# Sparse attention with a convolution between its steps: attention steps given priority in the scheduler, one softmax scaling moved from GpSimd to VectorE, the first stage scheduled by the framework, a narrower last piece

## The chip, the cores and the metric

One core of a Trainium2 chip. The time is the device time of one execution in microseconds. The engines are TensorE (PE, with its weight loads as PEld), VectorE (DVE), ScalarE (ACT), GpSimd (POOL) and SyncE (SP), which here issues the DMAs.

## The reference

One step of a decoder layer for 1024 prompt tokens and 8 sample tokens with 1024 features, all in float32:

```python
shift, scale, gate = split(silu(c) @ w_ada + b_ada)
h = rmsnorm(x, g_pre) * (1 + scale) + shift
z = h @ w_in                     # 5912 columns: q, kv, gates, za, conv (B, C, x), cg, merge
# branch A, per head group: compressed, selected (top 16 blocks) and sliding-window attention
o_cmp = masked_softmax(q @ kc.T) @ vc
o_sel = masked_softmax(q @ k_sel.T) @ v_sel
o_win = masked_softmax(q @ k_win.T) @ v_win
o_attn = g0 * o_cmp + g1 * o_sel + g2 * o_win
ya = (o_attn * silu(za)) @ w_br_a
# branch B: short gated convolution
yb = (cb * conv3(cc * cx) * silu(cg)) @ w_br_b
o = (sigmoid(ga) * ya + sigmoid(gb) * yb) @ w_out
y = x + gate * rmsnorm(o, g_post)
```

With 1024 keys the prompt has 16 blocks of 64, so all blocks up to the current one are selected. Outputs are y of prompt and sample, the key and value rows, the window rows and the convolution state.

## The kernel before, in words

A float32 product is made of three matmuls on rounded halves: an operand a is split into ah (rounded, `copy`, L110 or L112) and al = a - ah (`sub`, L115), and ah·bh + al·bh + ah·bl go into one PSUM bank (`mm`, L106). PSUM has eight banks of 512 columns in four groups: two "acc", three "S", two "T", one "O".

**First stage (0 to about 75 us).** x comes in eight tiles of 128 tokens. `norm_x` squares and sums a tile on ACT and takes the inverse root on POOL, `scale_x` (L337) multiplies it on DVE, `trans_x` (L349) transposes it on PE, `ada` and `ada_end` make the modulation from `w_ada` as its pieces land, and `make_h` (L387 to L390, L112, L115) writes the halves Hh and Hl, feature by feature, for which projection matmuls of 344 columns wait. Up to `in_order.__exit__` (L739) a manual schedule (L285) holds all five engines to the order in which the code is written. This includes the projections of keys, values and queries and the compression of keys and values (G, L636, is a transposed piece of it; X its operand).

**Attention (231 to 595 us).** There are 16 pairs (eight query tiles of 128 by two key groups) with two units each, branch 1 (the compressed keys together with the selected ones) and branch 2 (the window). A unit's `a_steps` multiply queries by keys into an "S" bank, take mask and maximum on DVE (L963), the exponential on ACT (L968), then the sums' inverses and gates (L974 to L976), and scale the weights P: for the compressed part one POOL multiply of 128x256 (L979), for the others one multiply a head on DVE (L987) or, for the last head of a long row, on ACT. Its `b_steps` transpose P on PE into a "T" bank (L1000 for the compressed part, L1014 for the others), split it (ph on ACT L110, pl on DVE L115; pc for the compressed part) and multiply by the values into the pair's "O" bank, first `pc`. At the end of a pair the two halves of "O" are added into QO (L1033), the upper half by way of an SBUF tile `ot`.

**The filling.** The projections of the gated convolution (`conv_tiles`, three of its four blocks, 288 steps of three matmuls of 344 columns into "acc") are given out between the attention's steps: the loop at L1053 to L1090 sorts the a_steps of one unit and the b_steps of the unit before by their planned times, and ahead of each step `advance` takes as many filling steps as its share of the planned total. The filling's DVE work is at L862 to L882. Its last evaluation (`e_cg`) writes an SBUF tile `ct`. `ot` and `ct` share one slot (tag "tmp", one buffer), so each of them waits for the user before it in program order. Here the framework's scheduler sets the order on every engine from its own estimates, with the program order as the priority.

**After attention.** The fourth convolution block, the gates, both branch products, then w_out in eight tiles of 128 tokens with 48 matmuls of 512 columns each, and `finish` (L1351 to L1366) for each: squares and their sums on ACT (L1358), y = o·GG on DVE (L1359), mean and epsilon (L1360, L1361), the power -0.5 on POOL (L1362), y·st + x on DVE (L1365), two stores of 512 columns.

Of the kernel before, what the change touches and what calls it, by code (L numbers as in the profile page):

```python
# [19 lines left out]
F32 = mybir.dt.float32  # L20
F32R = mybir.dt.float32r
I32 = mybir.dt.int32
AF = mybir.ActivationFunctionType
OP = mybir.AluOpType
# [61 lines left out]
def _build(ctx, tc, nc, I, O):  # L86
# [3 lines left out]
    def dma(out, in_):  # L90
        return nc.sync.dma_start(out, in_)
# [7 lines left out]
    def bank(tag):  # L99
        return psum.tile([128, 512], F32, name="ps" + tag, tag=tag, bufs=NB[tag])  # L100
# [174 lines left out]
    def load_x(t):  # L275
# [4 lines left out]
        else:  # L280
# [1 line left out]
            dma(x, I["x_sample"][:, 0, :])  # L282
        xs[t] = x

    in_order = tc.manual_schedule(engines={mybir.EngineType.PE, mybir.EngineType.DVE, mybir.EngineType.Activation,  # L285
                                           mybir.EngineType.Pool, mybir.EngineType.SP})
    in_order.__enter__()
    dma(ct[0:1, :], I["c_prompt"])
    dma(ct[1:9, :], I["c_sample"])
# [654 lines left out]
    def a_steps(u):  # L944
        u.P, u.mx, u.sm = {}, [], []
        for br, n in u.parts:
            u.P[br] = ap.tile([128, 4, (64, 1024, 640)[br]], F32, name=f"P{br}", tag=f"P{br}", bufs=1)
            u.mx.append(ap.tile([128, 4, 2], F32, name="mx", tag="mx", bufs=3))
            u.sm.append(ap.tile([128, 8], F32, name="sm", tag="sm", bufs=3))
        K = KS[u.br - 1][u.g]  # L950
        hh = QT[u.i]
        for j in range(4):
            seen = [0] * len(u.parts)
            for k0, nt, subs in u.ch:
                ps = bank("S")
                mm(ps[:, :nt], hh[u.g][:, j, :], K[:, k0:k0 + nt], True, False)
                mm(ps[:, :nt], QL[u.g][:, j, :], K[:, k0:k0 + nt], False, True)
                c0 = 0
                for x, o, n, m in subs:
                    (br, total_n), mx, sm = u.parts[x], u.mx[x], u.sm[x]  # L960
                    Pb, ci = u.P[br], seen[x]
                    init = 0.1 * BIG if ci == 0 else mx[:, j, (ci - 1) % 2:(ci - 1) % 2 + 1]
                    V.tensor_tensor_reduce(out=Pb[:, j, o:o + n], in0=ps[:, c0:c0 + n], in1=m, scale=1.0, scalar=init,  # L963
                                           op0=OP.add, op1=OP.min, accum_out=mx[:, j, ci % 2:ci % 2 + 1])
                    seen[x] += 1
                    c0 += n
                    if o + n == total_n:
                        A.activation(Pb[:, j, 0:total_n], Pb[:, j, 0:total_n], AF.Exp, bias=mx[:, j, ci % 2:ci % 2 + 1], scale=-1.0,  # L968
                                     accum_out=sm[:, j:j + 1])
                if j == 3 and (k0, nt, subs) == u.ch[-1]:  # L970
                    for x, (br, n) in enumerate(u.parts):
                        sm, Pb = u.sm[x], u.P[br]
                        if br == 0:
                            V.tensor_scalar(sm[:, 0:4], sm[:, 0:4], 1e-30, None, op0=OP.max)  # L974
                        V.reciprocal(sm[:, 4:8], sm[:, 0:4])
                        V.tensor_tensor(out=sm[:, 4:8], in0=sm[:, 4:8],  # L976
                                        in1=gate[:, u.i, 12 * u.g + br:12 * u.g + br + 10:3], op=OP.mult)
                        if br == 0:
                            P.tensor_tensor(out=Pb, in0=Pb, in1=sm[:, 4:8].rearrange("p (j o) -> p j o", o=1).to_broadcast(  # L979
                                [128, 4, 64]), op=OP.mult)  # L980
                            continue
                        for jj in range(4):
                            p = Pb[:, jj, 0:n]
                            if jj == 3 and n > 256:
                                A.activation(p, p, AF.Copy, scale=sm[:, 4 + jj:5 + jj])
                            else:
                                V.tensor_scalar(p, p, sm[:, 4 + jj:5 + jj], None, op0=OP.mult)  # L987
                yield max(0.22, 2 * nt * 0.00046)
# [71 lines left out]
    for n in range(len(units) + 1):  # L1060
# [20 lines left out]
        for k, (at, which, t) in enumerate(ev):  # L1081
            if u:
                advance(span * (at - past))
                past = at
            next(lb if which else la)
        if u:
            advance(span * (1 - past))
        for _ in la:
# [201 lines left out]
    gps = tp.tile([128, D], F32, name="gps")  # L1290
    src = I["g_post"]
    dma(gps, bass.AP(tensor=src.tensor, offset=src.offset, ap=[[0, 128], [1, D]]))
    for b in range(2):
        cs = slice(512 * b, 512 * b + 512)
        ps = bank("S")
        mm(ps, kr[:, 0:128], gs2[:, cs], True, True)
        V.tensor_tensor(out=GG[:, cs], in0=ps, in1=gps[:, cs], op=OP.mult)
        ps = bank("S")
        mm(ps[:NS, :], kr[:, 128:136], gs2[:, cs], True, True)
        V.tensor_tensor(out=GS[:, cs], in0=ps[:NS, :], in1=gps[:NS, cs], op=OP.mult)  # L1300
# [47 lines left out]

    ob = pool("ob", "left")

    def finish(ps, n, x, g, dst):  # L1351

        sq = ob.tile([128, 512], F32, name="sq", tag="sq", bufs=1)
        st = ob.tile([128, 4], F32, name="fst", tag="fst", bufs=2)
        y = ob.tile([128, D], F32, name="y", tag="y", bufs=2)
        for h in range(2):
            cs = slice(512 * h, 512 * h + 512)
            A.activation(sq[:n], ps[h][:n, :], AF.Square, accum_out=st[:n, h:h + 1])  # L1358
            V.tensor_tensor(out=y[:n, cs], in0=ps[h][:n, :], in1=g[:n, cs], op=OP.mult)  # L1359
        V.tensor_tensor(out=st[:n, 2:3], in0=st[:n, 0:1], in1=st[:n, 1:2], op=OP.add)  # L1360
        V.tensor_scalar(st[:n, 2:3], st[:n, 2:3], 1.0 / D, EPS, op0=OP.mult, op1=OP.add)  # L1361
        P.tensor_tensor(out=st[:n, 3:4], in0=st[:n, 2:3], in1=mhalf[:n], op=OP.pow)  # L1362
        for h in range(2):
            cs = slice(512 * h, 512 * h + 512)
            V.scalar_tensor_tensor(y[:n, cs], y[:n, cs], st[:n, 3:4], x[:n, cs], op0=OP.mult, op1=OP.add)  # L1365
            dma(dst[:, cs], y[:n, cs])  # L1366


    msr = ob.tile([128, KT, 40], F32R, name="msr")
# [45 lines left out]
    for t in range(8):  # L1415
        if t < 7:
            split_m(t + 1)
        mh, ml = mt.pop(t)
        tag = "S" if t % 2 else "acc"
        ps = [bank(tag), bank(tag)]  # L1420
        for k0, k1 in (((0, 7), (7, 8)) if t == 0 else ((0, 8),)):
            for h in range(2):
                cs = slice(512 * h, 512 * h + 512)
                for k in range(k0, k1):
                    mm(ps[h], mh[k], WOh[:, k, cs], k == 0, False)
                    mm(ps[h], mh[k], WOl[:, k, cs], False, False)
                    mm(ps[h], ml[k], WOh[:, k, cs], False, k == KT - 1)
        if t == 1:
            sample_out()
        finish(ps, 128, xt.pop(t), GG, O["y_prompt"][0, 128 * t:128 * t + 128, :])  # L1430


_INS = ['x_prompt', 'x_sample', 'cache_kv_pages', 'state_win_kv', 'state_conv', 'page_table', 'c_prompt', 'c_sample',
# [22 lines left out]
```

## Time and profile before

| | us |
|---|---|
| three runs | 1085.88, 1086.84, 1087.47 |
| median | 1086.84 |
| the profiled execution: its own time | 1087.87 |
| its span, first to last instruction | 1086.1 |
| mean granted clock of TensorE | 0.985 of 2.4 GHz |

The page of the profile gives each engine's busy time and, in 40 slices of the span (27.15 us each), its busy share in tenths. A matmul's records overlap the next one's, so a busy PE shows no idle time but not the rate either; the rate is read from how many matmuls start in a stretch. "Waits" list for which other engine's instruction an idle engine waited.

### The profile page before, as it was taken

How to read it: one execution, taken by the hardware profiler on the slowest of the kernel's cores; microseconds unless marked ns; L12 is line 12 of the kernel's file. 1: busy time of each engine (PE TensorE's matmuls, PEld its weight loads, DVE VectorE, ACT ScalarE, POOL GpSimd, SP SyncE). 2: the span in 40 equal slices, each digit the busy share in tenths (PEclk: the TensorE clock that was granted, in tenths of full speed). 3: DMA queues.
4: the chain of work that ended last, by engine and by line, in shares of the span. 5: the costliest groups of instructions: out<-in, count | busy, mean ns of one | idle time of the engine just before them, and what ended most of it. 6: DMA issues, size and time to landing. Idle time of an engine off the chain costs nothing.

```text
span 1086.1 us, 17011 instructions
## 1 busy us (share of the span) xinstructions
PE 1043.6 (96%) x6310; PEld 959.7 (88%) x6310; DVE 673.4 (62%) x1823; ACT 453.4 (42%) x1006; POOL 105.3 (10%) x106
## 2 busy tenths in 40 slices
PE   5898999999999999999999999999999999999997
PEld 4688999978888988888888999999999999998785
DVE  4676656457998898878987745344365311583432
ACT  5566533346787767776666011111012111121221
POOL 3100000122222121211111010000000000120000
PEclk8899999989999999999999999999999999999999
DMA  9752242210000000000001312442331121332222
GB/s 329 209 146 76 78 101 59 70 30 20 21 20 20 21 20 20 11 20 11 20 21 42 98 51 65 154 128 61 79 81 46 40 58 40 105 108 79 79 78 78
DMA packets 103408, 75.98 MB, mean 70 GB/s; under 512 B 23873, under 2 KB 92680, under 8 KB 103324
## 3 DMA queue, kind: packets, MB, share of 16 engines
q1 hardware_dynamic: 103324, 74.88, 24.3%
q8 instruction: 50, 0.82, 0.3%
q14 instruction: 34, 0.28, 0.1%
HBM read 65.85 MB, written 9.01 MB: 69 GB/s over the span
## 4 chain that ended last, share of the span: by engine, by line
PE 60%; DVE 2%; ACT 0%; issue 0%; DVEq 0%; POOLq 0%; ACTq 0%
PE psacc L106 38%; PE psS L106 13%; PE psO L106 4%; PE psT L1014 3%; PE psT L106 1%; DVE P L987 1%; DVE P L963 0%; DVE pl L115 0%; PE psT L1205 0%; PE psT L1000 0%; DVE YB L867 0%; DVE qh L112 0%; DVE sm L976 0%; DVE QO L1033 0%; ACT ph L110 0%
## 5 line engine op out<-in xcount | busy, mean ns | idle before, releaser
L106 PE MATMUL psacc<-Hh,wh 128*128 128x344 f32 x1072 | 353.4, 330 | 3.6 <-DVE Hh L112 3.6
L106 PE MATMUL psacc<-Hh,wl 128*128 128x344 f32 x1072 | 347.5, 324 | 1.0 <-DVE wl L115 1.0
L106 PE MATMUL psacc<-Hl,wh 128*128 128x344 f32 x1072 | 346.5, 323 | 0.0
L106 PEld LDWEIGHTS psacc<-Hh,wh 128*128 128x128 f32 x1072 | 203.8, 190 | 11.2 <-DVE Hh L112 4.0
L106 PEld LDWEIGHTS psacc<-Hl,wh 128*128 128x128 f32 x1072 | 203.5, 190 | 4.5 <-DVE Hl L115 0.5
L106 PEld LDWEIGHTS psacc<-Hh,wl 128*128 128x128 f32 x1072 | 203.9, 190 | 3.7 <-DVE wl L115 1.8
L968 ACT ACTIVATE P<-P,mx 128x64 f32<-128x64 f32 (+5 forms) x192 | 115.1, 601 | 41.6 <-DVE mx L963 40.4
L112 DVE CAST wh<-wraw 128x512 fp32r<-128x512 f32 x78 | 33.7, 437 | 121.7 <-PE psacc L106 115.4
L115 DVE TENSOR_TENSOR pl<-psT,ph 128x512 fp32r<-128x512 f32 x132 | 90.2, 688 | 16.0 <-ACT ph L110 14.0
L110 ACT ACTIVATE ph<-psT 128x512 fp32r<-128x512 f32 x132 | 77.6, 592 | 45.2 <-PE psT L1014 44.3
L115 DVE TENSOR_TENSOR wl<-wraw,wh 128x512 fp32r<-128x512 f32 x112 | 77.1, 693 | 28.6 <-ACT wh L110 24.3
L1014 PE MATMUL psT<-ident,P 128*128 128x128 f32 x528 | 87.6, 278 | 5.5 <-DVE P L987 5.1
L1014 PEld LDWEIGHTS psT<-ident,P 128*128 128x128 f32 x528 | 64.0, 141 | 20.4 <-issue 5.7
L963 DVE CUSTOM_DVE_ANT_0 P<-psS,kbig 128x64 f32<-128x64 f32 (+4 forms) x192 | 74.2, 409 | 11.7 <-PE psS L106 10.8
L106 PE MATMUL psS<-K,qh 128*128 128x384 f32 (+6 forms) x208 | 69.5, 335 | 2.4 <-DVE YB L872 1.7
L106 PE MATMUL psS<-K,ql 128*128 128x384 f32 (+6 forms) x208 | 69.2, 333 | 0.0
L115 POOL TENSOR_TENSOR wl<-wraw,wh 128x512 fp32r<-128x512 f32 x28 | 36.3, 1298 | 263.3 <-ACT wh L110 260.7
L106 PE MATMUL psO<-pl,V 128*128 128x512 f32 x132 | 60.5, 458 | 1.0 <-DVE pl L115 0.8
L110 ACT ACTIVATE wh<-wraw 128x512 fp32r<-128x512 f32 x62 | 38.9, 629 | 40.7 <-PE psS L106 20.3
L987 DVE TENSOR_SCALAR P<-P,sm 128x640 f32<-128x640 f32 (+7 forms) x104 | 53.3, 567 | 0.4
L106 PE MATMUL psO<-ph,V 128*128 128x512 f32 x132 | 52.7, 399 | 0.0
L1247 ACT ACTIVATE M<-psacc 128x344 f32<-128x344 f32 x24 | 11.0, 457 | 87.8 <-PE psacc L106 87.8
(344 smaller groups left out, 1743.7 us busy)
## 6 DMA issues: line engine op xcount, KB each, us to landing
wraw<-w_in SPq DMA_DIRECT2D x76, 256.0 KB
x<-x_prompt SPq DMA_DIRECT2D x8, 512.0 KB
x<-w_ada SPq DMA_DIRECT2D x16, 256.0 KB
ar<-w_ada SPq DMA_DIRECT2D x16, 256.0 KB
wraw<-w_in SPq DMA_DIRECT2D x32, 128.0 KB
wraw<-w_cmp SPq DMA_DIRECT2D x16, 256.0 KB
wraw<-w_ada SPq DMA_DIRECT2D x16, 256.0 KB
wor<-w_out SPq DMA_DIRECT2D x16, 256.0 KB
```

The lines of the kernel that those rows point to most:

```text
L106: PE.matmul(out, lhsT, rhs, start=start, stop=stop, skip_group_check=True)
L110: A.activation(out, in_, AF.Copy)
L112: eng.tensor_copy(out, in_)
L115: eng.tensor_tensor(out=out, in0=a, in1=b, op=OP.subtract)
L963: V.tensor_tensor_reduce(out=Pb[:, j, o:o + n], in0=ps[:, c0:c0 + n], in1=m, scale=1.0, scalar=init, op0=OP.add, op1=OP.min, accum_out=mx[ ...
L968: A.activation(Pb[:, j, 0:total_n], Pb[:, j, 0:total_n], AF.Exp, bias=mx[:, j, ci % 2:ci % 2 + 1], scale=-1.0, accum_out=sm[:, j:j + 1])
L987: V.tensor_scalar(p, p, sm[:, 4 + jj:5 + jj], None, op0=OP.mult)
L1014: PE.transpose(pt[:, j * 128:(j + 1) * 128], u.P[u.br][:, j, n * 128:(n + 1) * 128], ident)
L1247: A.activation(M[:, f, cs], acc, AF.Tanh, scale=0.5)
```

## The change

Four things, in a diff of some 60 lines:

1. The manual schedule of the first stage holds PE and SP alone. DVE, ACT and POOL are ordered there by the framework's scheduler.
2. In attention each step is made under `tc.high_priority(offset=240)`: its instructions count as written 240 earlier. The filling, called from `advance`, and the queries' splitting (`prep_q`) keep their places.
3. The compressed weights are scaled by DVE instead of POOL.
4. `finish`: the factor D of the mean is folded into g_post (one DVE multiply when g_post has come) and the small sums are joined, the power is issued ahead of the last y multiply, and the last tile (t = 7) is cut into pieces of 512, 256 and 256 columns instead of 512 and 512, with a third bank.

```diff
-    in_order = tc.manual_schedule(engines={mybir.EngineType.PE, mybir.EngineType.DVE, mybir.EngineType.Activation,
-                                           mybir.EngineType.Pool, mybir.EngineType.SP})
+    in_order = tc.manual_schedule(engines={mybir.EngineType.PE, mybir.EngineType.SP})
...
-                            P.tensor_tensor(out=Pb, in0=Pb, in1=sm[:, 4:8].rearrange("p (j o) -> p j o", o=1).to_broadcast(
+                            V.tensor_tensor(out=Pb, in0=Pb, in1=sm[:, 4:8].rearrange("p (j o) -> p j o", o=1).to_broadcast(
                                 [128, 4, 64]), op=OP.mult)
...
-            next(lb if which else la)
+            with tc.high_priority(offset=240):
+                next(lb if which else la)
...
+    V.tensor_scalar(gps, gps, float(D) ** 0.5, None, op0=OP.mult)
...
-    def finish(ps, n, x, g, dst):
+    def finish(ps, n, x, g, dst, cuts=(0, 512, 1024)):
...
+        for i, (a, b) in enumerate(zip(cuts, cuts[1:])):
+            o = ps[i][:n, 0:b - a]
+            A.activation(sq[:n, 0:b - a], o, AF.Square, accum_out=st[:n, i:i + 1])
+            if i == len(cuts) - 3:
+                s0 = st[:n, 0:1]
+                if i:
+                    V.tensor_tensor(out=st[:n, 4:5], in0=s0, in1=st[:n, 1:2], op=OP.add)
+                    s0 = st[:n, 4:5]
+            if i == len(cuts) - 2:
+                V.scalar_tensor_tensor(st[:n, 3:4], s0, D * EPS, st[:n, i:i + 1], op0=OP.add, op1=OP.add)
+                P.tensor_tensor(out=st[:n, 3:4], in0=st[:n, 3:4], in1=mhalf[:n], op=OP.pow)
+            V.tensor_tensor(out=y[:n, a:b], in0=o, in1=g[:n, a:b], op=OP.mult)
+        for a, b in zip(cuts, cuts[1:]):
+            V.scalar_tensor_tensor(y[:n, a:b], y[:n, a:b], st[:n, 3:4], x[:n, a:b], op0=OP.mult, op1=OP.add)
+            dma(dst[:, a:b], y[:n, a:b])
...
+        cuts = (0, 512, 768, 1024) if t == 7 else (0, 512, 1024)
```

What moves in the engines' orders. In the **first stage**, ACT ahead of the first transposes of the compression (G; xf and X are the operand's halves, QO a query projection, wh a weight). Before:

```order
L110 ACTIVATE xf<-kvraw 64x512 x2
L110 ACTIVATE X_878<-xf 128x8x64
L110 ACTIVATE xf<-kvraw 64x512 x2
L110 ACTIVATE X_878<-xf 128x8x64
L724 ACTIVATE QO<-psacc 128x344
L110 ACTIVATE wh<-wraw 128x512
L110 ACTIVATE G_1000<-x 128x2x2x64 x2
L110 ACTIVATE xf<-kvraw 64x512
```

With the change:

```order
L110 ACTIVATE xf<-kvraw 64x512 x2
L723 ACTIVATE QO<-psacc 128x344
L110 ACTIVATE X_878<-xf 128x8x64
L110 ACTIVATE G_1000<-x 128x2x2x64 x2
L110 ACTIVATE xf<-kvraw 64x512 x2
L110 ACTIVATE wh<-wraw 128x512
L110 ACTIVATE X_878<-xf 128x8x64
L110 ACTIVATE X_878<-psS 128x8x64
L110 ACTIVATE G_1038<-x 128x2x2x64
L110 ACTIVATE wh<-wraw 128x512
L723 ACTIVATE QO<-psacc 128x344
L110 ACTIVATE G_1038<-x 128x2x2x64
```

The first G stands ahead of the second pair of xf and of a weight; the second G is cut in two, around a weight and a query projection.

In **attention**, PE around the first product of the last pair (`psO<-pc`; psacc is the filling, psT transposes, psS queries by keys). Before:

```order
L1014 MATMUL psT<-ident,P_6370 128x128 x2
L106 MATMUL psacc<-Hh,wh 128x344
L106 MATMUL psacc<-Hl_601,wh 128x344
L106 MATMUL psacc<-Hh,wl 128x344
L106 MATMUL psacc<-Hh,wh 128x344
L106 MATMUL psS<-K_1835,qh_5976 128x384
L106 MATMUL psS<-K_1835,ql_2416 128x384
L106 MATMUL psacc<-Hl_606,wh 128x344
L106 MATMUL psacc<-Hh,wl 128x344
L106 MATMUL psO<-pc,vc 128x512
L1014 MATMUL psT<-ident,P_6370 128x128 x4
```

With the change:

```order
L106 MATMUL psacc<-Hl_601,wh 128x344
L106 MATMUL psacc<-Hh,wl 128x344
L106 MATMUL psacc<-Hh,wh 128x344
L106 MATMUL psacc<-Hl_606,wh 128x344
L106 MATMUL psacc<-Hh,wl 128x344
L106 MATMUL psacc<-Hh,wh 128x344
L106 MATMUL psO<-pc,vc 128x512
L106 MATMUL psO<-pl,V_1841 128x512
L106 MATMUL psO<-ph,V_1841 128x512
L106 MATMUL psO<-pl,V_1841 128x512
```

Here 110 matmuls of the filling stand in a row ahead of `psO<-pc`. Counted over the whole order, the filling's matmuls that stand ahead of each pair's `psO<-pc`:

| pair | 1 | 2 | 3 | 4 | 5 | 6 | 7 | 8 | 9 | 10 | 11 | 12 | 13 | 14 | 15 | 16 |
|---|---|---|---|---|---|---|---|---|---|---|---|---|---|---|---|---|
| before | 7 | 37 | 82 | 126 | 166 | 195 | 240 | 288 | 340 | 401 | 469 | 533 | 599 | 668 | 746 | 823 |
| change | 0 | 17 | 50 | 72 | 90 | 138 | 227 | 281 | 300 | 339 | 381 | 512 | 570 | 603 | 648 | 800 |

Before, they come in threes and sixes between the attention's steps. With the change four long rows of them stand alone: 36 and 79 ahead of pair 12, 29 ahead of pair 13, 110 ahead of pair 16, which is 254. On ACT the order of the users of slot "tmp" is the same in both kernels.

At the **end**, DVE after the last matmul (fst holds the sums). Before:

```order
L1359 TENSOR_TENSOR y<-psS,GG 128x512 x2
L1360 TENSOR_TENSOR fst<-fst 128x1
L1361 TENSOR_SCALAR fst<-fst 128x1
L1365 SCALAR_TENSOR_TENSOR y<-y,fst,xr 128x512 x2
```

With the change:

```order
L1370 TENSOR_TENSOR y<-psS,GG 128x512
L1364 TENSOR_TENSOR fst<-fst 128x1
L1370 TENSOR_TENSOR y<-psS,GG 128x256
L1368 SCALAR_TENSOR_TENSOR fst<-fst 128x1
L1370 TENSOR_TENSOR y<-psacc,GG 128x256
L1372 SCALAR_TENSOR_TENSOR y<-y,fst,xr 128x512
L1372 SCALAR_TENSOR_TENSOR y<-y,fst,xr 128x256 x2
```

Between the last square and the power there is one small operation instead of a wide and two small ones. Outside these places PE's order is that of before, from the start to attention and from there to the last tile.

## Rows read from the trace of the kernel before

**Rows 1.** The page of the profile: the span, PE's busy time, and the busy tenths in 40 slices of the span of PE, DVE and TensorE's granted clock.

```profile
span 1086.1 us, 17011 instructions
PE 1043.6 (96%) x6310; PEld 959.7 (88%) x6310; DVE 673.4 (62%) x1823; ACT 453.4 (42%) x1006; POOL 105.3 (10%) x106
...
PE   5898999999999999999999999999999999999997
...
DVE  4676656457998898878987745344365311583432
...
PEclk8899999989999999999999999999999999999999
```

**Rows 2.** Busy time by stretch over the attention (four stretches from 231 to 595 us; the first and the sum): length, then busy us and instructions of each engine, granted clock, DMA share, GB/s.

```profile
231.00:326.50 95.50, 87.11 (x511) 78.35 (x512) 84.63 (x325) 67.43 (x213) 22.01 (x21) 0.93 0.07 18
...
sum 364.00, PE 349.84 PEld 314.58 DVE 317.81 ACT 258.07 POOL 68.35; mean PE 87.46 PEld 78.64 DVE 79.45 ACT 64.52 POOL 17.09
```

**Rows 3.** The same view, stretches of 25 us at the start of attention and one late in it.

```profile
225.00:250.00 25.00, 22.57 (x124) 20.11 (x123) 19.43 (x88) 14.07 (x54) 6.27 (x6) 0.80 0.04 12
250.00:275.00 25.00, 22.80 (x138) 20.90 (x137) 20.59 (x84) 16.74 (x54) 4.92 (x5) 0.93 0.09 22
275.00:300.00 25.00, 22.70 (x141) 20.55 (x140) 24.42 (x85) 17.98 (x55) 6.59 (x6) 1.00 0.09 22
300.00:325.00 25.00, 23.41 (x146) 20.54 (x146) 23.62 (x80) 20.30 (x56) 5.45 (x5) 1.00 0.09 22
...
500.00:525.00 25.00, 24.42 (x150) 21.55 (x148) 23.40 (x65) 16.27 (x34) 4.47 (x4) 1.00 0.04 11
```

**Rows 4.** Groups of DVE instructions from 231 to 595 us by line and shape: the attention's split and mask, then the filling's seven groups.

```profile
L115 DVE TENSOR_TENSOR pl<-psT,ph 128x512 fp32r<-128x512 f32 x132 | 90.2, 688 | 16.0 <-ACT ph L110 14.0
L963 DVE CUSTOM_DVE_ANT_0 P<-psS,kbig 128x384 f32<-128x384 f32 x72 | 39.4, 551 | 5.0 <-PE psS L106 4.7
...
L867 DVE SCALAR_TENSOR_TENSOR YB<-u,prmT,YB 128x344 f32<-128x344 f32 x12 | 8.3, 689 | 0.0
...
L862 DVE TENSOR_TENSOR u<-psacc,u 128x344 f32<-128x344 f32 x9 | 4.6, 509 | 0.2
L877 DVE TENSOR_TENSOR YB<-psacc,YB 128x344 f32<-128x344 f32 x9 | 4.6, 508 | 1.0 <-PE psacc L106 0.9
L882 DVE SCALAR_TENSOR_TENSOR ct<-ct,psacc 128x344 f32<-128x344 f32 x9 | 4.6, 506 | 1.0 <-ACT ct L881 0.8
...
L867 DVE SCALAR_TENSOR_TENSOR YB<-u,prmT,YB 128x336 f32<-128x336 f32 x6 | 3.4, 560 | 0.0
...
L865 DVE TENSOR_SCALAR YB<-u,prmT 128x344 f32<-128x344 f32 x6 | 2.3, 389 | 0.0
L865 DVE TENSOR_SCALAR YB<-u,prmT 128x336 f32<-128x336 f32 x3 | 2.2, 749 | 0.0
```

**Rows 5.** Busy time by stretch again: two stretches at half the clock near the start of attention, and one of projection matmuls with no attention beside them.

```profile
233.90:244.10 10.20, 9.71 (x38) 8.35 (x38) 7.96 (x43) 6.54 (x29) 2.14 (x2) 0.50 0.01 2
254.30:257.80 3.50, 3.50 (x14) 3.31 (x13) 2.01 (x8) 1.72 (x6) 2.46 (x2) 0.51 0.31 74
...
650.00:660.00 10.00, 10.00 (x64) 9.41 (x64) 5.27 (x13) 0.38 (x1) 0.00 (x0) 1.00 0.37 100
```

**Rows 6.** The compressed weights' multiply on POOL, its group from 231 to 595 us.

```profile
L979 POOL TENSOR_TENSOR P<-P,sm 128x256 f32<-128x256 f32 x16 | 10.3, 643 | 98.5 <-DVE sm L976 46.8 <-PE psO L106 25.8 <-PE psacc L106 15.1
```

**Rows 7.** What PE waited for from 231 to 595 us: us in total, times, the longest.

```profile
PE psT L1014 <- DVE P L987: 5.1, 9, 1.1
...
PE psT L1000 <- POOL P L979: 2.3, 4, 0.9
```

**Rows 8.** DVE in order of time (start, duration): its multiplies of four heads, once with POOL idle and once beside it.

```profile
241.81 0.87 DVE L987 TENSOR_SCALAR P<-P,sm 128x128 f32<-128x128 f32 x4
...
248.44 2.23 DVE L987 TENSOR_SCALAR P<-P,sm 128x128 f32<-128x128 f32 x4
```

**Rows 9.** POOL in order of time beside the second of them.

```profile
248.29 0.62 POOL L979 TENSOR_TENSOR P<-P,sm 128x256 f32<-128x256 f32 x1 [8.87 <-DVE sm L975]
249.11 1.28 POOL L115 TENSOR_TENSOR wl<-wraw,wh 128x512 fp32r<-128x512 f32 x1 [0.20 <-ACT wh L110]
```

**Rows 10.** What PE waited for in the first 95 us, in part.

```profile
PE psS L636 <- ACT G L110: 2.6, 1, 2.6
```

**Rows 11.** DVE's scaling of the x tiles, its group in the first 75 us.

```profile
L337 DVE TENSOR_SCALAR x<-x,ss 128x1024 f32<-128x1024 f32 x8 | 6.0, 751 | 0.0
```

**Rows 12.** The end, in order of time: start, duration, engine, line, what is written and read, idle time before and who ended it.

```profile
1078.74 0.39 PE L106 MATMUL psS<-WOh,ml 128*128 128x512 f32 x1
1079.23 0.60 ACT L1358 ACTIVATE sq<-psS 128x512 f32<-128x512 f32 x1 [4.85 <-PE psS L106]
...
1079.95 0.69 DVE L1359 TENSOR_TENSOR y<-psS,GG 128x512 f32<-128x512 f32 x1 [4.85 <-ACT sq L1358]
1080.55 0.15 DVE L1360 TENSOR_TENSOR fst<-fst 128x1 f32<-128x1 f32 x1
1080.74 0.15 DVE L1361 TENSOR_SCALAR fst<-fst 128x1 f32<-128x1 f32 x1
1081.06 0.55 POOL L1362 TENSOR_TENSOR fst<-fst,mhalf 128x1 f32<-128x1 f32 x1 [10.69 <-DVE fst L1361]
1081.64 1.41 DVE L1365 SCALAR_TENSOR_TENSOR y<-y,fst,xr 128x512 f32<-128x512 f32 x2 [0.75 <-POOL fst L1362]
```

More of the change, by code (lines that the diff above doesn't have):

```diff
@@ L1349, in _build @@
     ob = pool("ob", "left")
-    def finish(ps, n, x, g, dst):
+    def finish(ps, n, x, g, dst, cuts=(0, 512, 1024)):
         sq = ob.tile([128, 512], F32, name="sq", tag="sq", bufs=1)
-        st = ob.tile([128, 4], F32, name="fst", tag="fst", bufs=2)
+        st = ob.tile([128, 5], F32, name="fst", tag="fst", bufs=2)
         y = ob.tile([128, D], F32, name="y", tag="y", bufs=2)
[L1356 to L1366, printed above, removed]
+        for i, (a, b) in enumerate(zip(cuts, cuts[1:])):
[13 more added lines that the diff above has]
+            dma(dst[:, a:b], y[:n, a:b])
     msr = ob.tile([128, KT, 40], F32R, name="msr")
@@ L1419, in _build @@
         tag = "S" if t % 2 else "acc"
+        cuts = (0, 512, 768, 1024) if t == 7 else (0, 512, 1024)
         ps = [bank(tag), bank(tag)]
+        if t == 7:
+            ps.append(bank("acc"))
         for k0, k1 in (((0, 7), (7, 8)) if t == 0 else ((0, 8),)):
-            for h in range(2):
-                cs = slice(512 * h, 512 * h + 512)
+            for i, (a, b) in enumerate(zip(cuts, cuts[1:])):
+                o, cs = ps[i][:, 0:b - a], slice(a, b)
                 for k in range(k0, k1):
-                    mm(ps[h], mh[k], WOh[:, k, cs], k == 0, False)
-                    mm(ps[h], mh[k], WOl[:, k, cs], False, False)
-                    mm(ps[h], ml[k], WOh[:, k, cs], False, k == KT - 1)
+                    mm(o, mh[k], WOh[:, k, cs], k == 0, False)
+                    mm(o, mh[k], WOl[:, k, cs], False, False)
+                    mm(o, ml[k], WOh[:, k, cs], False, k == KT - 1)
         if t == 1:
             sample_out()
-        finish(ps, 128, xt.pop(t), GG, O["y_prompt"][0, 128 * t:128 * t + 128, :])
+        finish(ps, 128, xt.pop(t), GG, O["y_prompt"][0, 128 * t:128 * t + 128, :], cuts)
 _INS = ['x_prompt', 'x_sample', 'cache_kv_pages', 'state_win_kv', 'state_conv', 'page_table', 'c_prompt', 'c_sample',
```

## The prediction

> **What bounds the kernel now.** I read the page first: PE is busy 96% of the span, DVE 62%, but DVE's tenths go from 4 to 7 in the first quarter to 8 and 9 in the slices of attention and back to 3 to 5 behind it [rows 1]. So the mean hides a stage in which two engines are full. The view by stretch gives that stage: of 364.0 us PE is busy 349.8 and DVE 317.8 [rows 2], which leaves PE 14.2 us and DVE 46.2 us idle. The 25-us stretches show where DVE's idle time lies: 10.0 us of it in the first 50 us (225 to 275), next to nothing from 275 to 300 (24.42 busy of 25.00), 1.4 in the stretch behind that [rows 3]. PE's best stretch there is also 24.42 of 25 [rows 3]. Both engines can thus run at up to 0.977, and neither has 4% to spare over the whole. What the change does in attention is decided by how evenly the filling, which is PE work with little DVE work, lies beside the attention, which is mostly DVE work.
>
> **The compressed weights on DVE.** Removed from POOL: 16 multiplies, 10.3 us [rows 6], and PE's waits for them, 2.3 us in four [rows 7]. Added to DVE: 16 operations of 128x256. Rows with 344 and 512 columns take 509 and 688 ns [rows 4], 1.065 ns a column, so 256 take 509 - 88 x 1.065 = 415 ns, 6.6 us in all. DVE also gains: four multiplies that take 0.87 us with POOL idle took 2.23 beside it [rows 8]; 1.36 us were lost to 0.47 us of L979 and 1.28 us of another POOL instruction [rows 9], 0.78 us for each us beside POOL, so 0.36 for this L979 and 5.8 if all 16 stood like this. None need to; I take the middle, 2.9 (ends 0 and 5.8). DVE's work becomes 317.8 + 6.6 - 2.9 = 321.5 us. PE's 2.3 us turn into waits for the same weights from DVE, and are counted in DVE's rate below.
>
> By the Trainium skill ("SBUF — State Buffer", section "Who interferes with whom") a DVE operation with two inputs in SBUF contends with a POOL instruction that reads SBUF, and a `tensor_scalar` can contend as well, the later one being held for the whole of the other. By that rule the new multiply can itself be held by POOL's splits, against the change; and at its best all 10.3 us of POOL come back to DVE, so that it would have 314.1 us and the sum would be 7.7 lower, about PE's fast end below. The 1.36 us lost in one place agree that something is lost, not that all of it is.
>
> **Priority in attention.** The order has the attention about one unit further ahead of the filling at the start, and four long rows of filling alone, 254 matmuls, because `ot` waits for `ct` in one slot. I build the stage's time from DVE:
>
> - DVE's work at the rate of 275 to 325, where attention is dense: 24.42 + 23.62 of 50 is 0.961 [rows 3]; 321.5 / 0.961 = 334.5 us.
> - The long rows. Projection matmuls alone start 64 in 10.00 us [rows 5], 0.156 each; 254 take 39.7 us. The filling's seven DVE groups sum to 30.0 us [rows 4] for 864 / 24 = 36 steps of 24 matmuls, 0.83 each, so 254 / 24 x 0.83 = 8.8 us of DVE's work lies in these rows and 30.9 us are left. At the start of each row DVE can have behind it what three "S" banks and two "T" banks hold: 3 x 0.551 + 2 x 0.688 = 3.0 us [rows 4], in four rows 12.1. Idle time: 18.8 us (ends 0 and 30.9).
> - The start. Of the 10.0 us idle from 225 to 275, 2.0 are in the rate already. Attention now has PE to itself up to its first `psO<-pc` (0 filling matmuls instead of 7, then 17 instead of 37), so DVE is fed earlier, but the chain from matmul to exponential to weights is as long as before: between 3 and 8.0 us stay, I take the middle, 5.5.
>
> Sum 334.5 + 18.8 + 5.5 = 358.8 against 364.0: **-5.2 us**. The fast end is PE's: its 349.8 us hold 13.2 us at half the clock (0.50 and 0.51 of 2.4 GHz) [rows 5], which would be 6.6 at full clock, so 343.2 / 0.977 = 351.3, -12.7. The slow end has no catching up and the start as before: 334.5 + 30.9 + 8.0 = 373.4, +9.4.
>
> What else waits behind these: the queries' splitting keeps its low priority, so the lead of the attention ends where it needs the next query tile; and SP's and POOL's loads and weight splits for the filling come in the same sequence, needed later, never earlier. I cost them at nothing; what hides them is the filling's own lag, and without it each filling step waits for a weight's split of 1.28 us on POOL [rows 9].
>
> **First stage.** PE waits 2.6 us for the first G [rows 10]. ACT now makes it ahead of two pieces of xf and a weight, but the second G is cut around a weight and a query projection, so part of the wait comes back there. I take -1.1 (ends -2.6 and 0). The reordered norms and scalings mostly go where PE waits for pieces of w_ada anyway; the one price I see is a scaling of 0.75 us [rows 11] that DVE now does ahead of a half that a projection needs. I cost it at nothing, cover being the transfers, and +0.75 if they are not late. SP's order, which starts the transfers, hardly moves.
>
> **The end.** From the last matmul on, in sequence: square 0.60, y 0.69, two small sums (1080.55 to 1081.06, 0.51), power 0.55, two last operations 1.41 [rows 12]. With the change: a square of 256 columns (0.2 less, an estimate between its 0.60 for 512 and a fixed part), one small sum (0.32, so 0.19 less), y of 256 columns beside the power instead of ahead (0.60 less, 1079.95 to 1080.55), three last operations instead of two (0.75 + 2 x 0.42 = 1.59, 0.18 more). Together -0.8; a third store may take the gain of a smaller last transfer or 0.5 us more, ends -1.3 and +0.2. The one added DVE multiply on g_post lies in a stage where DVE is a third busy [rows 1].
>
> **Sum.** -5.2 - 1.1 - 0.8 = -7.1 us on the profiled execution's own 1087.87: 1080.8. That execution stands 1.0 above the median of the three runs, so against 1086.84 I predict **1080 us**.
>
> **Rivals.**
>
> 1. *The lead is paid back at the shared slot (slower).* DVE finds nothing left over when a long row of filling starts, because the attention's last transposes and scores before it have been drained while their weights were awaited, and all 30.9 us are idle: 334.5 + 30.9 + 5.5 = 370.9, +6.9 in the stage, +5.0 with the other terms, 1091.8. The point: the stage loses once DVE idles more than 364.0 - 334.5 - 5.5 = 24.0 us in the long rows, the kernel from 25.9. For it: the longest row is 110 matmuls or 17 us, many times the 3.0 us that the banks hold. Against it: where filling is missing, PE has room, and attention might run at over 0.961.
> 2. *It only moves waits (no change).* Both engines are within 4 to 13% of the stage's length now, and PE's order has the same matmuls. If gain at the start and loss in the long rows cancel and the G is hidden by the next one, the end alone remains: 1086.84 - 0.8 = 1086.0, or 1085 with the first stage.
> 3. *The clock.* TensorE was at half its clock for 13.7 us near the start of attention [rows 5]. With the filling held back, PE has more short idle times just there. If it stays at 1.2 GHz for as long again, that costs 6.6 us: 1086.4 in place of 1080, and 1093 if three times as long. The Trainium skill ("TensorE: Matmul & The Clock Gate", section "A second HAM failure mode: psum-queue depth-cycling") tells of short idle times between groups of matmuls that send the clock up and down between its levels. The trace agrees with two such falls at the start of attention, while the later stretches shown have 1.00 [rows 3].
>
> **How the numbers follow.** About 0.2%, 2.2 us, is what a measurement of this kernel can tell from no change, so "same" is 1084.7 to 1089.0. Forecast, with 1070 to 1084.7 as its own range: 0.50. Rival 1: 0.28. Rival 2: 0.14. Rival 3: 0.08, half of it on the slow side. Faster 0.50, same 0.14 + 0.04 = 0.18, slower 0.28 + 0.04 = 0.32. Low end: 1086.84 - 12.7 - 2.6 - 1.3 = 1070.2. The high end by the bounds is 1086.84 + 9.4 + 0.75 + 0.2 = 1097.2; I stop at 1093, which takes in rivals 1 and 3.
>
> **What would show it.** Right: the stage from the first `psO<-pc` to the last sum into QO is about 5 us shorter, DVE idles some 19 us in the four long rows of filling and is above 0.95 busy elsewhere; L1000's wait for POOL is gone; the first G's transposes come 1 to 3 us earlier; the last matmul to the end is 0.8 us shorter. Wrong: DVE idle above 26 us in the long rows (rival 1), a stage of 364 us with other waits (rival 2), a granted clock below 0.93 in the first 95 us of attention (rival 3; it was 0.93 [rows 2]), or attention that runs above 0.977 of DVE, which would break my fast end.

## The result, and the profile after

The changed kernel is slower: 1102.88 us median (1097.81 to 1104.24, four runs) against 1087.15 (four runs of before), ratio 1.0131, 95% interval 1.0104 to 1.0157. The forecast was 1080 with a range to 1093. The profiled execution took 1102.0 us.

The page of the changed kernel, lines as in [rows 1]:

```profile
span 1100.2 us, 17046 instructions
...
PE 1053.7 (96%) x6334; PEld 964.6 (88%) x6334; DVE 672.1 (61%) x1834; ACT 450.0 (41%) x1008; POOL 93.8 (9%) x90
...
PE   5899999989999999999999999999999999999997
...
DVE  4675755389998899588984734434456321484423
...
PEclk8999999989999999999999999999999999999999
```

The whole page gives PE the same 96%. The difference is in DVE's tenths: where before has an unbroken run of 7 to 9 through attention, there are now a 5 and, at its end, a 4. Those slices hold most of the long rows of filling.

Attention lies from 227.8 to 610.4 us, which is 382.6 us where before had 364.0 [rows 2]; the start is 3.2 us earlier, so this stage alone lost 18.6. Busy time by stretch (first stretch and sum of six):

```profile
227.80:323.30 95.50, 87.20 (x503) 75.51 (x503) 88.82 (x354) 71.82 (x229) 15.82 (x12) 0.93 0.05 12
...
sum 382.60, PE 361.63 PEld 318.75 DVE 320.76 ACT 257.27 POOL 59.78; mean PE 60.27 PEld 53.12 DVE 53.46 ACT 42.88 POOL 9.96
```

The first stretch, as long as the first of [rows 2], has 4.2 us more of DVE's work in it: the lead is real. The same view of the four long rows of filling shows where it goes:

```profile
443.60:449.40 5.80, 5.80 (x38) 5.76 (x38) 5.71 (x18) 0.83 (x1) 0.00 (x0) 1.00 0.01 3
450.70:463.80 13.10, 12.65 (x80) 12.36 (x79) 2.44 (x6) 2.76 (x6) 3.52 (x3) 1.00 0.17 40
486.40:493.20 6.80, 5.15 (x30) 4.58 (x30) 4.66 (x10) 3.00 (x10) 2.40 (x3) 1.00 0.13 36
571.00:589.70 18.70, 18.17 (x112) 17.89 (x111) 5.99 (x15) 3.15 (x5) 3.52 (x3) 0.97 0.12 29
sum 44.40, PE 41.78 PEld 40.58 DVE 18.79 ACT 9.74 POOL 9.45; mean PE 10.44 PEld 10.14 DVE 4.70 ACT 2.44 POOL 2.36
```

DVE idles 25.6 of 44.4 us here, in the second and fourth row for most of their length (10.7 of 13.1 and 12.7 of 18.7 us), while PE is busy with the filling. What the attention waits for is read at the end of the second row (in order of time, all engines; most of the filling's matmuls left out):

```profile
460.09 0.46 ACT L880 ACTIVATE ct<-psacc 128x344 f32<-128x344 f32 x1 [3.25 <-PE psacc L106]
...
460.58 0.51 DVE L881 SCALAR_TENSOR_TENSOR ct<-ct,psacc 128x344 f32<-128x344 f32 x1 [3.75 <-ACT ct L880]
...
461.18 0.93 POOL L882 TENSOR_TENSOR YB<-ct,YB 128x344 f32<-128x344 f32 x1 [2.95 <-DVE ct L881]
...
462.13 0.60 ACT L110 ACTIVATE ot<-psO 64x512 f32<-64x512 f32 x1 [1.58 <-POOL YB L882]
...
462.76 0.68 DVE L1032 TENSOR_TENSOR QO<-psO,ot 64x512 f32<-64x512 f32 x1 [1.67 <-ACT ot L110]
...
463.50 0.50 PE L106 MATMUL psO<-pc,vc 128*128 128x512 f32 x1 [0.45 <-DVE QO L1032]
```

This is the slot "tmp" at work. `ot` may not be written until POOL has read the filling's `ct`; `ct` needs the end of an accumulation on PE; and until `ot` and the sum into QO are done, the one "O" bank is taken, so the next pair's `psO<-pc` stands. A finished attention pair waits for a filling that is far behind it. The waits by engine say the same. ACT has a wait for the slot, which before does not have:

```profile
ACT ot L110 <- POOL YB L882: 10.3, 6, 3.9
```

PE has one behind it, for the sum into QO (first row), which before does not have either. Two more of PE's waits grew, for the masks (0.4 us before) and for the compressed weights (2.3 us before [rows 7]), but the longest of each, 2.3 and 2.2 us, has another cause, told below; its waits for `pc` fell from 3.1 to 1.0 us:

```profile
PE psO L106 <- DVE QO L1032: 2.7, 4, 1.3
PE psS L106 <- DVE mx L962: 2.7, 3, 2.3
PE psT L999 <- DVE P L978: 2.6, 2, 2.2
```

The clock falls more often, too. Attention had two stretches of half clock before, both at its start [rows 5]; now it has one there (10.2 us) and four behind it (window, busy times, granted clock in the third column from the end):

```profile
281.97:285.38 3.41, 3.15 (x12) 2.51 (x11) 3.27 (x10) 1.69 (x4) 1.05 (x1) 0.50 0.00 0
353.65:357.06 3.41, 3.41 (x15) 3.32 (x14) 2.45 (x14) 2.76 (x9) 0.08 (x1) 0.50 0.08 24
493.60:497.01 3.41, 3.41 (x13) 2.93 (x12) 1.29 (x2) 1.15 (x3) 0.00 (x0) 0.50 0.00 0
568.69:572.10 3.41, 3.41 (x14) 3.35 (x15) 3.41 (x12) 1.74 (x3) 0.00 (x0) 0.50 0.29 74
```

12 to 15 matmuls of mixed widths fall into each, where 3.4 us of filling at full clock hold 22 (64 in 10.00 us [rows 5]). Three of the four come within 1.2 us behind a gap of PE of 1.3 us or more; the last section shows that such a gap is not always followed by a fall.

**An account on PE.** The stage is best measured to the last `ct` of the convolution, so that the filling left over at attention's end is in it. The same view, from the first score matmul to there, before and after:

```profile
231.10:635.90 404.80, 390.74 (x2408) 355.37 (x2409) 342.85 (x1090) 263.41 (x635) 70.11 (x65) 0.98 0.10 26
```
```profile
228.20:650.80 422.60, 401.75 (x2410) 358.70 (x2409) 343.50 (x1106) 260.75 (x635) 61.25 (x49) 0.97 0.10 25
```

17.8 us longer with the same PE instructions and 0.7 us more on DVE. Before, PE idled 14.1 us and was 13.7 at half clock; after, 20.9 and 23.9. Taking half clock at half its length, 6.8 us are idle time and 5.1 the clock; the other 5.9 are hidden by the overlapping matmul records. Read from start to start of the matmuls, the time lost at full clock against each width's usual spacing grew from 40.6 to 53.0 us, an estimate; these 12.4 us are about the 6.8 and the 5.9 together.

**First stage and end.** PE's wait for G is 1.7 us in two instead of 2.6 in one [rows 10]:

```profile
PE psS L635 <- ACT G L110: 1.7, 2, 1.0
```

and the end, lines as in [rows 12], takes 6.3 us from the last matmul's start to the end of the span instead of 7.4:

```profile
1093.87 0.28 PE L106 MATMUL psacc<-WOh,ml 128*128 128x256 f32 x1
1094.24 0.39 ACT L1359 ACTIVATE sq<-psacc 128x256 f32<-128x256 f32 x1 [2.34 <-PE psacc L106]
...
1094.75 0.16 DVE L1368 SCALAR_TENSOR_TENSOR fst<-fst 128x1 f32<-128x1 f32 x1 [2.32 <-ACT sq L1359]
1094.83 0.42 DVE L1370 TENSOR_TENSOR y<-psacc,GG 128x256 f32<-128x256 f32 x1
1095.05 0.55 POOL L1369 TENSOR_TENSOR fst<-fst,mhalf 128x1 f32<-128x1 f32 x1 [10.49 <-DVE fst L1368]
1095.64 1.54 DVE L1372 SCALAR_TENSOR_TENSOR y<-y,fst,xr 128x512 f32<-128x512 f32 x3 [0.39 <-POOL fst L1369]
```

### The profile page after: what moved, and what is told of

The parts are those of the page before. It is cut to its first block, busy times and chain, and to the rows that moved or that the text cites. A ratio compares the mean times of both kernels' runs of the same rounds, so it can differ in the third digit from the quotient of the medians.

```text
span 1100.2 us, 17046 instructions
## 1 busy us (share of the span) xinstructions
PE 1053.7 (96%) x6334; PEld 964.6 (88%) x6334; DVE 672.1 (61%) x1834; ACT 450.0 (41%) x1008; POOL 93.8 (9%) x90
## 3 DMA queue, kind: packets, MB, share of 16 engines
q1 hardware_dynamic: 103468, 74.88, 23.9%
## 4 chain that ended last, share of the span: by engine, by line
PE 54%; DVE 3%; ACT 0%; issue 0%; POOL 0%; POOLq 0%; DVEq 0%; ACTq 0%
PE psacc L106 36%; PE psS L106 11%; PE psO L106 3%; PE psT L1013 2%; DVE P L962 1%; PE psT L106 1%; DVE P L986 1%; PE psT L1205 0%; DVE pl L115 0%; DVE QO L1032 0%; POOL YB L882 0%; ACT ot L110 0%; DVE qh L112 0%; DVE pc L115 0%; ACT P L967 0%
## 5 line engine op out<-in xcount | busy, mean ns | idle before, releaser
L967 ACT ACTIVATE P<-P,mx 128x64 f32<-128x64 f32 (+8 forms) x192 | 114.7, 600 | 30.6 <-DVE mx L962 29.7
L1013 PE MATMUL psT<-ident,P 128*128 128x128 f32 x528 | 90.7, 282 | 6.0 <-DVE P L986 3.3
L106 PE MATMUL psS<-K,qh 128*128 128x384 f32 (+6 forms) x208 | 72.6, 352 | 4.9 <-DVE mx L962 2.7
L106 PEld LDWEIGHTS psS<-K,qh 128*128 128x128 f32 x208 | 40.7, 196 | 13.2 <-DVE mx L962 6.0
```

Source lines behind the costliest of these rows:

```text
L106: PE.matmul(out, lhsT, rhs, start=start, stop=stop, skip_group_check=True)
L1013: PE.transpose(pt[:, j * 128:(j + 1) * 128], u.P[u.br][:, j, n * 128:(n + 1) * 128], ident)
```

## The experiments

Sixteen kernels ran, in four groups. Ratios are to the kernel before on the same chips, with 95% intervals; the us behind them are ratio minus one times 1088. Stage, PE idle and half clock are those of the account above, from each kernel's own profile.

| kernel | ratio (interval) | us | stage | PE idle | half clock |
|---|---|---|---|---|---|
| before | 1 | 0 | 404.8 | 14.1 | 13.7 |
| changed | 1.0131 (1.0104 to 1.0157) | +14.3 | 422.6 | 20.9 | 23.9 |
| e1 changed, no priority | 0.9949 (0.9937 to 0.9961) | -5.5 | 402.4 | 12.6 | 10.2 |
| e2 before + priority | 1.0104 (1.0089 to 1.0120) | +11.3 | 417.7 | 18.5 | 23.9 |
| e3 changed, no shared slot | 0.9990 (0.9982 to 0.9999) | -1.1 | 406.6 | 14.5 | 13.7 |
| e4 changed, priority 60 | 0.9974 (0.9965 to 0.9983) | -2.8 | 405.6 | 15.1 | 10.2 |
| e5 before + weights on VectorE | 0.9978 (0.9968 to 0.9987) | -2.4 | 402.8 | 13.6 | 10.2 |
| e6 before + first stage | 0.9963 (0.9949 to 0.9976) | -4.0 | 404.9 | 14.1 | 13.7 |
| e7 before + end | 0.9991 (0.9982 to 1.0000) | -1.0 | 405.0 | 14.1 | 13.7 |
| e8 e1, no shared slot | 0.9937 (0.9924 to 0.9950) | -6.9 | 402.8 | 12.3 | 13.7 |
| e9 e8 + rows by hand | 0.9959 (0.9946 to 0.9973) | -4.5 | 403.7 | 15.6 | 6.8 |
| e10 e8, filling thinned | 0.9979 (0.9969 to 0.9989) | -2.3 | 405.1 | 15.6 | 6.8 |
| e11 changed, weights on GpSimd | 1.0058 (1.0046 to 1.0070) | +6.3 | 416.3 | 18.5 | 20.5 |
| e12 changed, priority 20 | 0.9915 (0.9903 to 0.9928) | -9.2 | 399.6 | 10.7 | 6.8 |
| e13 e3 + rows by hand | 1.0032 (1.0020 to 1.0045) | +3.5 | 412.1 | 18.6 | 13.7 |
| e14 e3, weights on GpSimd | 1.0003 (0.9994 to 1.0011) | +0.3 | 408.3 | 16.2 | 13.7 |
| e15 e12, no shared slot | 0.9924 (0.9908 to 0.9940) | -8.3 | 399.4 | 11.0 | 6.8 |
| e16 e12, weights on GpSimd | 0.9971 (0.9960 to 0.9983) | -3.2 | 407.2 | 16.2 | 13.7 |

**Which part: e1, e2.** e1 takes the priority out of the changed kernel, e2 puts it alone into the kernel before.

```diff
-            with tc.high_priority(offset=240):
-                next(lb if which else la)
+            next(lb if which else la)
```

> The changed kernel with the attention's steps at normal priority; the rest of the change stays. Theory A (the priority makes the loss): about 1083 us, 4 below before, since the first stage gained 3.2 us in the changed kernel's profile and the end about 0.8. Rival B (the compressed weights on VectorE make it): 1095 or more.

> The kernel before with the priority alone. Its order has the same long rows of filling as the changed kernel (298 matmuls in rows of 15 and more, 294 there). Theory A: about 1105 us, 18 above before, the whole loss of the attention stage. Rival B: within 4 us of before.

Measured: 1082.03 (-5.5 us) and 1100.14 (+11.3). The priority makes the loss; the rest of the change is a gain. The weights on VectorE, rival B, don't make it alone. But the loss is 11.3 us on the kernel before and 14.3 + 5.5 = 19.8 with the rest: something else in the change makes the priority worse.

**Slot or thin cover: e3, e4.** In e3 `ct` goes into the part of the filling's own tile u that nothing reads any more, so `ot` has the slot to itself; in e4 the priority is 60.

```diff
-            t = sp.tile([128, 512], F32, name="ct", tag="tmp", bufs=1)[:, 0:CH]
+            t = u[:, 2 + cs.start:2 + cs.stop]
```

> The changed kernel, but the filling's ct is written into the part of its own tile u that is no longer read, so that ot and ct share no slot. The order then has one row of 19 filling matmuls and no longer one; 627 instead of 800 filling matmuls stand ahead of the last pair's first product, the rest come behind attention. Theory A1 (the shared slot pays the lead back in the long rows, where VectorE idles 26 us): 1082 to 1088 us. Rival A2 (the attention without filling beside it has too many short gaps on TensorE, and the clock falls, wherever the filling stands): 1095 or more, with four or more stretches at half the clock in attention.

> The changed kernel with a priority of 60 instead of 240. The order has one row of 21 filling matmuls and no longer one, but attention still leads at the start (0, 17, 50 filling matmuls ahead of the first three pairs). Theory A1: 1080 to 1088 us. Rival A2: about half of the loss, 1094 or more.

Measured: 1086.47 and 1084.75, as A1 expected. The slot's edit alone gives back 15.4 us of the 19.8. It takes away two things at once, the waits at the slot and the long rows that the order had because of them. What is left of the loss is about what the lead itself costs: e3 stands 5.8 us above e8, the same kernel without the priority. The stage of e3:

```profile
228.40:635.00 406.60, 392.09 (x2408) 355.08 (x2409) 343.44 (x1106) 259.05 (x635) 59.77 (x49) 0.98 0.10 26
```

PE is idle 14.5 us and 13.7 at half clock, as before. With only 627 filling matmuls ahead of the last pair, attention ends 38 us earlier (last product of values at 564.9 instead of 602.9), and the filling left over takes that back.

**The other parts alone, and a control: e5 to e8.** e5, e6 and e7 each put one of the diff's other parts into the kernel before; e8 is e1 with e3's edit.

> The kernel before with the compressed weights scaled by VectorE, alone. By my term VectorE has 3.7 us more to do (bounds +0.8 to +6.6) and TensorE loses a wait of 2.3 us: between -2 and +4 us. Rival (the port's rule, all of POOL's 10.3 us come back): -4 us or more.

> The kernel before with the first stage ordered by the framework on VectorE, ScalarE and GpSimd, alone. By my term -1.1 us (bounds -2.6 to +0.75); by the landmarks of the changed kernel's profile (the compressed values' halves at 160.3 instead of 163.5 us) -3.2 us.

> The kernel before with the narrower last piece and the shorter chain of sums, alone. By my term -0.8 us (bounds -1.3 to +0.2); nothing in attention moves.

> The changed kernel without the priority and with ct in the filling's own tile. A control of the edit of the slot: without the priority no attention waits long for ct, so by theory A1 the slot is worth nothing here: 1081 to 1083 us like the kernel without the priority. If it is 3 us or more faster than that, the slot itself held something up in the kernel before too, and the gain of the slot's edit under the priority is not the long rows' alone.

Measured: -2.4, -4.0, -1.0 us, sum -7.4, where e1 has all three and -5.5; the intervals are 1 to 1.5 us wide on either side, so that of e7 reaches to 0. e8 stands 1.4 us from e1, inside the intervals: without the priority nobody waits long for the slot.

**Rows without the wait: e9, e10, e13.** Is it the wait at the slot, or that the filling spent in long rows is missing elsewhere? e9 and e13 give the filling out unevenly in kernels without the shared slot, e9 without priority, e13 with it (there in four rows of 30, 70, 10 and 70 steps); e10 only holds 98 steps back to the end.

```diff
+    ROWS = ((0.555, 38), (0.645, 10), (0.928, 37))
...
-        while state["f"] < NFILL * min(1.0, state["t"] / total) - 1e-6:
+        x = state["t"] / total
+        while state["f"] < (NFILL - 85) * min(1.0, x) + sum(r for at, r in ROWS if x >= at) - 1e-6:
```

> No priority and no shared slot (the kernel of 1081.8 us), but the filling is given out unevenly by hand: 38, 10 and 37 steps at once ahead of pairs 11, 13 and 16, the rest evenly. Its order has rows of 98, 18 and 98 filling matmuls and leaves the attention about as thinly covered elsewhere as the changed kernel (17, 49, 89 matmuls ahead of pairs 2 to 4). Theory C (what costs is that the filling in the long rows is missing beside the attention, where TensorE then has gaps and half clock): 1092 us or more, TensorE's gaps and half clock 8 us or more above the kernel without rows. Rival D (what costs is attention queued behind ot on ScalarE while the slot is held, as the changed kernel's waits of 10.3 us suggest; no such wait here): 1086 or less.

> No priority and no shared slot, with the filling thinned evenly: 98 of its 288 steps are held back to the end, so 562 instead of 814 matmuls stand ahead of the last pair's first product, in no long row. By theory C cover is worth less when it is thinned evenly than when it is missing in whole stretches: 1084 to 1089 us. If thin cover costs by its amount alone, it is as slow as the kernel with rows, 1092 or more.

> The changed kernel without the shared slot (1086.5 us), with the filling given out unevenly by hand, so that the lead of priority 240 and long rows (63 and 118 filling matmuls, 772 ahead of the last pair's first product) come together as in the changed kernel, but without the wait of ot for ct. Theory D (the wait at the slot, which holds ot, the single O bank and what is queued behind them, makes the loss): 1085 to 1090 us. Rival E (the lead and the long rows together do, slot or not): 1096 or more.

Measured: e9 1083.92, 2.4 us above e8: theory C, that the missing cover makes the loss, falls for a kernel without the lead. e10 1085.98, 4.6 above e8, in its range, but by the medians worse than the rows that C held to be worse (the intervals overlap a little). e13 1092.09, between the two theories' ranges, 4.6 us above e3:

```profile
228.90:641.00 412.10, 393.48 (x2410) 354.60 (x2409) 338.67 (x1106) 261.16 (x635) 59.14 (x49) 0.98 0.10 25
```

So with the lead, rows of 63 and 118 cost 4.6 us without any wait at the slot, and the changed kernel's rows with it 15.4. The rows aren't the same in both (254 matmuls in four there, 181 in two here), so the share of the wait, about 10 us, is an estimate, and it holds only with the weights on VectorE (see e11 and e14).

**The weights under the priority: e11, e14, e16.** Back on GpSimd in the changed kernel, in e3 and in e12.

```diff
-                            V.tensor_tensor(out=Pb, in0=Pb, in1=sm[:, 4:8].rearrange("p (j o) -> p j o", o=1).to_broadcast(
+                            P.tensor_tensor(out=Pb, in0=Pb, in1=sm[:, 4:8].rearrange("p (j o) -> p j o", o=1).to_broadcast(
```

> The changed kernel with the compressed weights back on GpSimd. The priority alone cost 12.5 us, the rest of the change gained 5.6, yet together they are 15 above before instead of 7. If the weights on VectorE turn into a loss under the priority (VectorE is asked for them ahead of its queue): 1095 to 1098 us. If they gain 2.4 us here as they do alone: 1105.

> The changed kernel without the shared slot and with the compressed weights on GpSimd. With the slot shared GpSimd was 8.3 us faster than VectorE. If that difference hangs on the waits at the slot, VectorE is the better place again here: 1087 to 1090 us. If the priority itself makes the weights on VectorE a loss: 1078 to 1082 us.

> The priority of 20 with the compressed weights on GpSimd. If VectorE gains 2.4 us as it does without any priority: 1081 to 1082 us. If it already loses under a small lead: 1077 or less.

Measured: 1094.60 (e11), 1088.37 (e14) and 1084.94 us (e16). The move to VectorE gains 2.4 us without priority (e5), 6.0 at priority 20 (e12 against e16, more than either expectation had), 1.4 at 240 without the shared slot (e3 against e14, intervals that overlap a little), and loses 7.9 at 240 with it (changed against e11). At 240 the loss appears only where the slot is shared. But the length of the waits at the slot does not measure it. ACT's wait there, 10.3 us in the changed kernel, is in e11 and then in e4

```profile
ACT ot L110 <- POOL YB L882: 11.9, 6, 3.9
```
```profile
ACT ot L110 <- POOL YB L882: 7.6, 6, 2.2
```

and yet the slot's edit gives back 6.0 us with the weights on GpSimd (e11 against e14) and 15.4 with them on VectorE, and e4, which has no row longer than 21, stands 2.7 us from e1. PE's longest wait for the weights is no example of the slot either: in pair 4 the multiply is queued on DVE behind another unit's mask, the sum into QO and a head's scaling, but `ot` did not wait for its slot there, and e3, which shares no slot, has the same wait and a fall of the clock behind it. In the changed kernel and in e3:

```profile
281.25 0.49 PE L999 MATMUL psT<-ident,P 128*64 128x128 f32 x3 [2.17 <-DVE P L978]
```
```profile
281.67 0.49 PE L999 MATMUL psT<-ident,P 128*64 128x128 f32 x3 [2.17 <-DVE P L978]
```

So it is shown that priority, shared slot and weights on VectorE together make the loss; by which waits on PE the last two add up to 7.9 us stays open.

**A small lead: e12, e15.** The priority is 20.

> The changed kernel with a priority of 20: no long row, a lead of a few filling steps (1, 25, 63 matmuls ahead of the first three pairs, 806 ahead of the last). By theory C a lead is worth nothing, since TensorE sets the time: 1082 to 1084 us, between the kernel without the priority (1082.0) and the one with 60 (1084.8). A faster result than 1081 would show that a small lead helps.

> The priority of 20 (1079.2 us) and no shared slot. With so small a lead ot waits little for ct: by theory D 1078 to 1080 us, no difference that can be measured. If it is faster by 2 us or more, the slot costs something even there.

Measured: e12 1079.20 us, the fastest of all, 2.8 below e1 by the medians and below the range expected: a small lead helps. The order has no long row, and PE idles least:

```profile
228.00:627.60 399.60, 388.87 (x2410) 351.91 (x2409) 346.04 (x1107) 261.27 (x635) 60.85 (x49) 0.99 0.10 26
```

Without the shared slot (e15) it is the same within the intervals, as expected: in e12 ACT waits 3.5 us for the slot.

## Why the prediction was wrong

- **The bound.** "I build the stage's time from DVE" is the step that failed. The prediction said that neither engine "has 4% to spare over the whole"; by its own rows that holds for PE alone, since DVE idled 46.2 of 364.0 us, 13%. In the table, stage less PE's idle time less half of its half clock is 383.7 to 386.7 us in the fifteen kernels that lack the shared slot or the priority of 240; the three that have both, e2, e11 and the changed kernel, have 387.3, 387.6 and 389.8. PE's work is fixed, and what varies is mostly what interrupts it: 20.9 us in before (14.1 + 6.8), 14.1 in e12, 32.9 in the changed kernel. I had those 20.9 us in hand, as PE's 14.2 idle and 6.6 of clock, but used them only for the fast end. The question to ask of the order was which PE gaps it opens, not how full DVE can be.
- **The rate beside the rows.** I priced DVE's work at 0.961, read where attention was dense and covered with filling [rows 3], and 5.5 us for the start: 18.5 us idle outside the long rows. Measured, 338.2 us outside the rows with 301.97 busy, 0.893 where I had named 0.95 as a sign of being right, and 36.2 idle. This term is 17.7 us of the 23.8 by which the stage missed (358.8 forecast, 382.6).
- **The long rows.** 18.8 us of DVE idle were forecast, with rival 1 from 24.0 and 30.9 at most; 25.6 were measured, just short of the 26 that I had named as rival 1's sign: by my own sum the rows alone would have left the kernel where it was. The direction was that of rival 1, and e3 shows that the shared slot has a large part in it. But its price, +5.0, was a third of the loss: it counted the idle time in the rows alone, and had nothing for the lead itself (5.8 us without the slot, e3 against e8) nor for what the slot and the weights on VectorE cost together. I also ended the range at 1093, below the 1097.2 of my own bounds; the result is above both.
- **The clock.** Rival 3 had 8% and a price of 6.6 for 13.7 us more; 10.2 us more came, 5.1 us. Its sign did not come: the granted clock of the first 95.5 us is 0.93 again, and the three added falls lie behind them. They came on top of rival 1, where I held the cases apart, and all three are gone without the slot (of the four falls behind the start, e3 has the first alone, at 282.1 us). The Trainium skill ("TensorE: Matmul & The Clock Gate", section "A second HAM failure mode: psum-queue depth-cycling") tells of short idle times between groups of matmuls, frequent enough to send the clock down and up; the trace agrees in part, with gaps of 2.17, 2.31 and 1.30 us ahead of three of the four falls and none above 0.6 us in the 70 us ahead of the fourth.
- **The weights on VectorE.** DVE's work rose by 2.9 us (317.8 to 320.8), with +3.7 forecast; in e5, where the move stands alone, it rose by 2.3 in the account's stage (342.8 to 345.1). As a part alone it gained 2.4 us (e5), just beyond the fast end of what was expected. In e5's profile the stage is 2.0 us shorter, 0.5 of it PE's idle time and 1.7 the clock, so it is not shown that the gain comes of the waits for POOL that PE no longer has. Under the priority and with the shared slot it cost 7.9, which no term had.
- **First stage and end.** -1.1 forecast, -4.0 measured (e6, 2.6 to 5.5 by its interval), beyond my bounds or at their end. The profiles agree: the first score matmul starts at 226.0 to 230.3 us in the fourteen kernels with the new order of the first stage, on average at 228.0, and at 230.4 to 233.6 in the four without it, on average at 231.8. In the changed kernel's profile the first G's transposes start at 81.7 us instead of 85.9, 4.2 earlier where the one wait I priced was 2.6 us, so work ahead of G gained too; which, no run tells apart. The end, -0.8 forecast, -1.0 measured (e7); by the traces 1.1.

## What to carry to other kernels

Where two engines are full, take the one whose work is fixed and ask which gaps of it a change opens or closes; a rate read from a stretch with cover does not hold where the change takes the cover away. Before one stream of work is given priority over another, look for tiles and banks that both use in turn: a single buffer in program order ties the fast one to the slow one, and here the tie cost more than the lead could bring (a lead of 20 gained 2.8 us, one of 240 lost 19.8, and 15.4 of these came back with the tie cut). The tie is not all of it: without it the long lead still lost 5.8 us, and with the weights on GpSimd the tie was worth 6.0 and not 15.4, so parts of a change that gain alone have to be measured together.

## What the runs showed of the hardware

- Half clock came behind short gaps, but not behind each of them. A gap of PE of 2.17 us that ended at 281.25 was followed by 1.2 GHz from 281.97, one of 2.31 us that ended at 352.45 from 353.65, one of 1.30 us that ended at 492.90 from 493.60, each for 3.4 us. A gap of 1.56 us in the same execution, at 443.38, was followed by 2.4 GHz up to 493.60:

```profile
443.38 0.42 PE L106 MATMUL psacc<-Hh,wh 128*128 128x344 f32 x1 [1.56 <-DVE u L861]
```
```profile
443.40:493.60 50.20, 47.83 (x285) 42.88 (x286) 33.57 (x96) 25.10 (x55) 9.68 (x8) 1.00 0.09 22
```

  In e11 one of 1.91 us that ended at 306.60 was followed by 2.4 GHz up to 435.9. The mean granted clock of one kernel also differs between its executions, from 0.980 to 0.986 in the four of the changed kernel, whose times spread from 1104.24 to 1097.81 us. What decides whether a gap brings a fall, no run here shows.
- A scaling on DVE beside GpSimd's weight splits can take far more than its time. In the changed kernel

```profile
348.52 3.40 DVE L986 TENSOR_SCALAR P<-P,sm 128x512 f32<-128x512 f32 x3
...
348.94 2.70 POOL L115 TENSOR_TENSOR wl<-wraw,wh 128x512 fp32r<-128x512 f32 x2 [3.11 <-ACT wh L110]
...
352.45 0.39 PE L106 MATMUL psS<-K,qh 128*128 128x256 f32 x1 [2.31 <-DVE mx L962]
```

  three heads took 3.40 us, where three of the same width took 1.27 in the kernel before with POOL idle:

```profile
349.09 1.27 DVE L987 TENSOR_SCALAR P<-P,sm 128x512 f32<-128x512 f32 x3
```

  The first of the three took 0.49 us, the second 1.60 and the third 1.48, and each of these two ended 0.28 us after a split had ended (350.53 after 350.25, 351.93 after 351.65). Behind them the masks were late, PE stood 2.31 us, and the clock fell at 353.65. The Trainium skill ("SBUF — State Buffer", section "Who interferes with whom") says that a `tensor_scalar` and a GpSimd instruction can contend, and that the later one is then blocked for the whole of the other; this place agrees.
